# Low parts of the MLP's middle tiles on VectorE, and a quad's second pair of raw weights in the square tiles

## The chip, the cores and the metric

The kernel runs on one core of a Trainium2 chip. The metric is the device time of one launch in microseconds; the median of several runs counts. A core has TensorE (PE), which multiplies; VectorE (DVE), ScalarE (ACT) and GpSimd (POOL), which work elementwise; and SyncE (SP), which here only issues DMAs. POOL issues DMAs too: those that add into their target.

## The reference

Two layers of a decoder trunk on x (512 positions, 1024 features), all in float32:

```
for l in range(2):
    h = rms_norm(x, norm_mix_g[l])
    proj = h @ w_in[l]                      # then attention, short convolution, RWKV-7
    x = x + mixed @ w_out[l]
    h = rms_norm(x, norm_mlp_g[l])
    x = x + jnp.square(jax.nn.relu(h @ w_mlp_up[l])) @ w_mlp_down[l]    # 1024 -> 4096 -> 1024
return rms_norm(x, final_norm_g)
```

The change lies in the two lines of the MLP alone.

## The kernel before

Activations lie transposed: features on the 128 partitions, the 512 positions along the free axis, so x is eight tiles `x[j]` of 128x512. Every operand of a product is split into a high part (`hi`, a cast to the reduced format that PE multiplies, made by ACT) and a low part (`lo` = value - `hi`, made by DVE or POOL), and a product of two operands is three matmuls: hi*hi, hi*lo, lo*hi.

A layer has a mixing stage, whose order is written out by hand (`ORDER`) and which the change does not touch, and then the MLP. In the MLP a scheduler sets the order of each engine's instructions; every engine takes its own in that order. Tiles come from rings: a tag with `bufs` buffers, used in turn, where a new tile waits until the readers of the one that lay there before are done.

The MLP has 32 middle tiles (`mids`, 128 rows of the 4096 each). `up` makes the first four, `two(i0, i1)` makes two at a time by a Strassen-like scheme of seven products (p1 to p7) on half-size operands. Its sums of weights come by DMA: SP loads one block into `s` (L1476), POOL adds the other to it by an accumulating DMA (L1477). The products share banks: p1 goes to bank `pa`, is copied out by ACT (L1523, tile `p`), and p6, the third product, adds into the same bank. `square` and `kept` then finish a middle tile: DVE scales with the norm and clips (L1418), ACT squares (L1419) and casts to `mh` (L1409), and `ml` is the low part (L1410).

`down(h, js)` multiplies middle tiles 4h to 4h+3 with w_mlp_down and adds to x; it is called for each h in two halves, js = 0..3 and 4..7, alternating with the `two`s. There are three ways of it:

- plain (h = 0, 7, and some others): four `dn` products, weights through `weights` (ring `raw`, cast to `whi`, low part `wlo`, rings of WB = 3), the result added into x by DVE (L1683);
- for h in `BY_DMA` = (1, 3, 5) the odd j of it: ACT copies the result to a tile `dx` of tag `sq` (L1680), and POOL adds it into x by DMA (L1681). `sq`, with two buffers, is the tag that holds the squares of the norm elsewhere;
- for the halves in `DN_QUADS` (h = 2, 4, 6 in layer 0, h = 2, 4 in layer 1, both halves each, ten calls) `quad`, a scheme of products p1, p2, ... for two pairs of output tiles. For each pair i it loads two raw weight tiles `rawq` (ring `raw`), casts `whi`/`wlo` of them, and forms sums `s2q`, `s4q` of them, with `shi`/`slo`. Its products go to banks `qa`, `qb`, `qc`; ACT copies them out as `p1q`, `p5q`, `u2q`, `c1q` (L1600), and the next product into `qa` waits for `p1q`. One result goes into x by DMA (L1646, tile `c0q`).

So each quad group runs: last half of a plain `down` with dx tiles (h odd), `two`, quad half 0, `two`, quad half 1, `two`, `down` of the next h.

Of the kernel before, what the change touches and what calls it, by code (L numbers as in the profile page):

```python
# [10 lines left out]
F32 = mybir.dt.float32  # L11
# [5 lines left out]
ALU = mybir.AluOpType  # L17
# [6 lines left out]
P = 128  # L24
# [250 lines left out]
def tile_trunk(ctx: ExitStack, tc: tile.TileContext, xT, wts, prm_d, cst_d, lora_d, gup_d, lam_d, fin_d, hd_d, out):  # L275
    nc = tc.nc
    act, dve, pool = nc.scalar, nc.vector, nc.gpsimd
# [23 lines left out]
    wp = Pool(ctx.enter_context(tc.tile_pool(name="wp", bufs=2)), "wp")  # L301
# [3 lines left out]
    def psum(tag, bufs, name):  # L305
        return ps.tile([P, 512], F32, tag=tag, bufs=bufs, name=name)
# [23 lines left out]
    WB = 3  # L330
# [238 lines left out]
    for l in range(L):  # L569
# [826 lines left out]
        with ExitStack() as mx:  # L1396
# [7 lines left out]
            def kept(m):  # L1404

                i = len(mids)
                hi = fp.tile([P, S], F32R, tag="mh", bufs=RING, name=f"mh{l}_{i}")
                lo = fp.tile([P, S], F32R, tag="ml", bufs=RING, name=f"ml{l}_{i}")
                act.copy(hi, m)  # L1409
                (dve if i < 4 else pool).tensor_tensor(lo, m, hi.bitcast(F32), ALU.subtract)  # L1410
                mids.append((hi, lo))

            def square(cs, name, side=ALU.max):

                m = fp.tile([P, S], F32, tag="m", bufs=4, name=f"m{name}")
                for i, c in enumerate(cs):
                    q = slice(i * H, i * H + c.shape[1])
                    dve.scalar_tensor_tensor(m[:, q], c, 0.0, rs[:, q], side, ALU.mult)  # L1418
                act.activation(m, m, AF.Square)  # L1419
                kept(m)  # L1420
                return m
# [152 lines left out]
            def quad(h, half):  # L1574
# [3 lines left out]
                def split(src, pool_, tags, bufs, name):  # L1578
                    hi, lo = [pool_.tile([P, 4, P], F32R, tag=t, bufs=bufs, name=f"{t}{l}_{h}_{name}")[:, :src.shape[1]] for t in tags]
                    act.copy(hi, src)  # L1580
                    dve.tensor_tensor(lo, src, hi.bitcast(F32), ALU.subtract)
                    return hi, lo
# [23 lines left out]
                for i in range(2):  # L1606
                    j = 4 * half + 2 * i
                    n = f"{l}_{h}_{j}"
                    r0, r1 = [wp.tile([P, 4, P], F32, tag="raw", bufs=WB, name=f"rawq{n}_{c}") for c in range(2)]
                    for c, r in enumerate((r0, r1)):  # L1610
                        nc.sync.dma_start(r.rearrange("p k c -> p (k c)"),
                                          wts[wbase + NG_IN + NG_OUT + NG_UP + 8 * g + j + c, :, k0 * P:(k0 + 4) * P])
                    w0 = split(r0, wp, ("whi", "wlo"), WB, f"{j}a")
                    s = [fp.tile([P, 4, P], F32, tag=t, name=f"{t}q{n}") for t in ("s2", "s4")]
                    dve.tensor_tensor(s[0][:, :2], r1[:, 0::2], r1[:, 1::2], ALU.add)
                    dve.tensor_tensor(s[0][:, 2:], s[0][:, :2], r0[:, 0::2], ALU.subtract)
                    s12 = split(s[0], fp, ("shi", "slo"), 5, f"{j}b")
                    dve.tensor_tensor(s[1][:, :2], r0[:, 0::2], r1[:, 0::2], ALU.subtract)
                    dve.tensor_tensor(s[1][:, 2:], r0[:, 1::2], s[0][:, 2:], ALU.subtract)
                    s34 = split(s[1], fp, ("shi", "slo"), 5, f"{j}c")  # L1620
                    w22 = split(r1[:, 1::2], wp, ("whi", "wlo"), WB, f"{j}d")
                    pts = [psum(t, b, f"q{c}{n}")[:, :H] for c, t, b in zip("abc", (("rp", "rp", "at"), ("mm", "mm", "at"))[i],
                                                                          ((4, 4, 2), (2, 2, 2))[i])]
                    ab.append((j, w0, s12, s34, w22, pts))
                for step in ((0, 1), (2, 3), (5, 4), (6,)):
                    for j, w0, s12, s34, w22, (pa, pb, pc) in ab:
                        n = f"{l}_{h}_{j}"
# [28 lines left out]
            def down(h, js):  # L1656

                if (h, js[0] // 4) in DN_QUADS[l]:
                    quad(h, js[0] // 4)
                    return  # L1660
                g, k0 = h // 2, 4 * (h % 2)
                if h == 0 and js[0] == 0:
                    pts = [psum(("at", "mm")[j], 2, f"dn{l}_{h}_{j}") for j in js[:2]]
                    ws = [list(weights(wbase + NG_IN + NG_OUT + NG_UP + 8 * g + j, k0, k0 + 4)) for j in js[:2]]
                    for a, b in ((0, 3), (3, 4)):
                        for j, pt, w in zip(js, pts, ws):
                            for k in range(a, b):
                                (whi, wlo), (ahi, alo) = w[k], mids[k]
                                pe.matmul(pt, whi, ahi, start=(k == 0), stop=False)
                                pe.matmul(pt, whi, alo, start=False, stop=False)  # L1670
                                pe.matmul(pt, wlo, ahi, start=False, stop=(k == 3))
                    for j, pt in zip(js, pts):
                        dve.tensor_tensor(x[j], pt, x[j], ALU.add)
                    js = js[2:]
                for j in js:
                    pt = psum(*(("mm", 2), ("rp", 4))[j % 2], f"dn{l}_{h}_{j}")
                    mm3(pt, weights(wbase + NG_IN + NG_OUT + NG_UP + 8 * g + j, k0, k0 + 4), mids[4 * h:4 * h + 4], 4)
                    if j % 2 and h in BY_DMA:
                        t = wp.tile([P, S], F32, tag="sq", bufs=2, name=f"dx{l}_{h}_{j}")
                        act.copy(t, pt)  # L1680
                        pool.dma_start(x[j], t, accum_op=ALU.add)  # L1681
                    else:
                        dve.tensor_tensor(x[j], pt, x[j], ALU.add)  # L1683
                    if h == 2 * N_KG - 1 and j < NK - LATE:
                        norm_tile(j, f"m{l + 1}")
# [92 lines left out]
```

## Time and profile before

| | us |
|---|---|
| runs | 1240.45, 1240.89, 1245.29; median 1240.89 |
| profiled execution | 1243.22 |
| its span, first to last instruction | 1241.4 |
| PE busy | 1220.0 (98%) |
| DVE busy | 987.5 (80%) |
| ACT busy | 754.1 (61%) |
| POOL busy | 425.2 (34%) |
| mean granted PE clock | 0.995 |

The MLP of layer 0 lies at about 299 to 620 us, that of layer 1 at about 900 to 1241. Busy shares are means over stages; a wait of PE is what costs time. PE's matmuls are pipelined: a 128x256 matmul is shown with 0.28 us, but in an unbroken row the next one starts 0.119 us later (0.227 for 128x512). A row of the timeline has the start in us, the duration in us, engine, line, operation, output and inputs, and in brackets the engine's idle time before it with what ended it. In the list of waits the numbers are us in total, times, and the longest in us. The issue of a DMA and its landing are told apart: `us to landing` counts from the issue.

### The profile page before, as it was taken

The numbers are of one execution on the slowest core, as the hardware profiler recorded it, in microseconds if no ns is written. First come the engines' busy times: TensorE is split into PE (matmuls) and PEld (weight loads), VectorE is DVE, ScalarE is ACT, GpSimd is POOL, SyncE is SP. The second block draws the span as 40 slices with busy tenths as digits, with TensorE's granted clock in tenths as the row PEclk, the third lists the DMA queues.
The fourth block names the chain that finished last, engine by engine and source line by source line (L and its number), as shares of the span: only waits on it lengthen the run. The fifth ranks groups of instructions, "written<-read, shape, count | busy, mean of one in ns | idle before, by whom it ended". The sixth has DMA issues, their size and how long they took to land.

```text
span 1241.4 us, 27076 instructions
## 1 busy us (share of the span) xinstructions
PE 1220.0 (98%) x10090; PEld 1068.4 (86%) x10090; DVE 987.5 (80%) x1979; ACT 754.1 (61%) x1630; POOL 425.2 (34%) x546
## 2 busy tenths in 40 slices
PE   9999999999999999999999999999999999999997
PEld 7888788888989989889888888888889898999987
DVE  7787888879788988888866777787897889787654
ACT  7785755557566656556675656564675566665543
POOL 2264636331133332231126454554202323223111
PEclk9999999999999999899999999999999999999999
DMA  6523323135664775743335243322455656658322
GB/s 225 159 90 109 115 82 106 51 106 154 195 162 121 186 171 131 183 112 83 105 113 158 82 133 112 96 72 69 142 174 145 164 152 176 155 135 204 77 78 77
DMA packets 101844, 160.04 MB, mean 129 GB/s; under 512 B 23248, under 2 KB 27088, under 8 KB 101712
## 3 DMA queue, kind: packets, MB, share of 16 engines
q1 hardware_dynamic: 87168, 132.39, 33.8%
q0 software_dynamic: 13824, 25.17, 12.5%
q8 instruction: 79, 1.29, 0.5%
q10 hardware_dynamic: 720, 0.75, 0.2%
q14 instruction: 53, 0.43, 0.1%
HBM read 137.56 MB, written 9.18 MB: 118 GB/s over the span
## 4 chain that ended last, share of the span: by engine, by line
PE 87%; DVE 6%; ACT 3%; DMA 2%; issue 2%; POOLq 0%; POOL 0%; ACTq 0%; DVEq 0%
PE pj L288 22%; PE dn L288 14%; PE pa L288 12%; PE po L288 8%; PE pb L288 6%; PE qa L288 4%; PE dnF L288 4%; PE pc L288 3%; PE up L288 2%; PE qb L288 2%; PE sc L288 1%; DMA raw<-wts 1%; PE ptt L293 1%; PE pg L288 1%; DMA rawq<-wts 1%
## 5 line engine op out<-in xcount | busy, mean ns | idle before, releaser
L695 POOL TENSOR_TENSOR wlo<-raw,whi 128x512 fp32r<-128x512 f32 x84 | 112.4, 1339 | 198.1 <-ACT whi L683 164.6
L288 PE MATMUL pj<-ahim,whi 128*128 128x512 f32 x392 | 156.8, 400 | 0.0
L288 PE MATMUL pj<-ahim,wlo 128*128 128x512 f32 x392 | 156.4, 399 | 0.2 <-issue 0.2
L288 PE MATMUL pj<-alom,whi 128*128 128x512 f32 x392 | 156.0, 398 | 0.0
L683 ACT CAST whi<-raw 128x512 fp32r<-128x512 f32 x142 | 87.6, 618 | 70.6 <-PE pj L288 27.0
L1410 POOL TENSOR_TENSOR ml<-m,mh 128x512 fp32r<-128x512 f32 x56 | 82.8, 1529 | 131.3 <-ACT mh L1409 62.9
L1477 POOL DMA_DIRECT2D s<-wts x52 | 47.5, 914 | 222.2 <-DVE slo_p L1492 67.6
L288 PE MATMUL dn<-ml,whi 128*128 128x512 f32 x288 | 112.5, 391 | 0.3 <-DVE ml L1410 0.3
L288 PE MATMUL dn<-mh,whi 128*128 128x512 f32 x288 | 112.4, 390 | 0.2 <-ACT mh L1409 0.2
L288 PE MATMUL dn<-mh,wlo 128*128 128x512 f32 x288 | 112.2, 390 | 0.0
L1491 ACT CAST shi_p<-s 128x512 fp32r<-128x512 f32 x112 | 69.6, 621 | 56.6 <-PE pa L288 37.6
L288 PE MATMUL pa<-thi,shi_p 128*128 128x256 f32 x336 | 95.4, 284 | 1.8 <-ACT p L1523 1.6
L1492 DVE TENSOR_TENSOR slo_p<-s,shi_p 128x512 fp32r<-128x512 f32 x112 | 76.9, 694 | 25.2 <-ACT shi_p L1491 23.7
L288 PE MATMUL pa<-tlo,shi_p 128*128 128x256 f32 x336 | 94.8, 282 | 0.0
L288 PE MATMUL pa<-thi,slo_p 128*128 128x256 f32 x336 | 94.3, 281 | 0.0
L350 DVE TENSOR_TENSOR wlo<-raw,whi 128x512 fp32r<-128x512 f32 x86 | 71.1, 830 | 22.1 <-ACT whi L349 22.1
L288 PEld LDWEIGHTS pj<-alom,whi 128*128 128x128 f32 x392 | 73.9, 188 | 14.0 <-issue 0.5
L288 PEld LDWEIGHTS pj<-ahim,wlo 128*128 128x128 f32 x392 | 73.8, 188 | 13.8 <-issue 0.2
L288 PEld LDWEIGHTS pj<-ahim,whi 128*128 128x128 f32 x392 | 73.9, 188 | 13.7 <-issue 0.3
L349 ACT CAST whi<-raw 128x512 fp32r<-128x512 f32 x86 | 53.1, 619 | 51.5 <-PE dn L288 24.6
L1491 ACT CAST shi_p<-raw 128x512 fp32r<-128x512 f32 x84 | 52.2, 621 | 38.1 <-PE pb L288 19.5
L288 PEld LDWEIGHTS pa<-thi,shi_p 128*128 128x128 f32 x336 | 62.9, 187 | 3.0 <-ACT p L1523 2.7
(651 smaller groups left out, 3932.7 us busy)
## 6 DMA issues: line engine op xcount, KB each, us to landing
raw<-wts SPq DMA_DIRECT2D x323, 256.0 KB, 2.8
s<-wts SPq DMA_DIRECT2D x52, 256.0 KB, 3.6
s<-wts POOLq DMA_DIRECT2D x52, 256.0 KB, 4.6
rawq<-wts SPq DMA_DIRECT2D x40, 256.0 KB, 2.8
x<-dx POOLq DMA_DIRECT2D x24, 256.0 KB, 4.0
x<-c0q POOLq DMA_DIRECT2D x20, 256.0 KB, 4.2
qs<-dqhi SPq DMA_DIRECT2D x24, 128.0 KB, 3.3
ks<-dkhi SPq DMA_DIRECT2D x24, 128.0 KB, 3.6
```

Source lines behind the costliest of these rows:

```text
L288: ins = nc.tensor.matmul(*a, **k)
L293: ins = nc.tensor.transpose(*a, **k)
L349: act.copy(hi[:, :n], raw[:, :n])
L350: (pool if a and lean[0] else dve).tensor_tensor(lo[:, :n], raw[:, :n], hi[:, :n].bitcast(F32), ALU.subtract)
L683: yield act.copy(hi[:, k0:k1], raw[:, k0:k1])
L695: yield eng.tensor_tensor(lo[:, k0:k1], raw[:, k0:k1], hi[:, k0:k1].bitcast(F32), ALU.subtract)
L1410: (dve if i < 4 else pool).tensor_tensor(lo, m, hi.bitcast(F32), ALU.subtract)
L1477: pool.dma_start(t.rearrange("p k c -> p (k c)"), of[1], accum_op=ALU.add)
L1491: act.copy(hi, src)
L1492: dve.tensor_tensor(lo, src, hi.bitcast(F32), ALU.subtract)
```

## The change

Two lines change. The low part of every middle tile is now made by DVE (before: of the first four only). In a quad, the raw weights of the second pair (i = 1) come from the tag `sq` with its two buffers, and those of the first pair stay in `raw` with three. The additions into x by DMA stay as they are.

```diff
@@ kept
                 act.copy(hi, m)
-                (dve if i < 4 else pool).tensor_tensor(lo, m, hi.bitcast(F32), ALU.subtract)
+                dve.tensor_tensor(lo, m, hi.bitcast(F32), ALU.subtract)
                 mids.append((hi, lo))
@@ quad
                 for i in range(2):
                     j = 4 * half + 2 * i
                     n = f"{l}_{h}_{j}"
-                    r0, r1 = [wp.tile([P, 4, P], F32, tag="raw", bufs=WB, name=f"rawq{n}_{c}") for c in range(2)]
+                    r0, r1 = [wp.tile([P, 4, P], F32, tag=("raw", "sq")[i], bufs=(WB, 2)[i], name=f"rawq{n}_{c}") for c in range(2)]
```

The scheduler answers with another order on SP, ACT, DVE and POOL; PE's order is the same. In the rows below the layer's number is cut from the names and a running number is added: `rawq_2_4_0_5778` is the first raw tile (c = 0) of quad h = 2, pair j = 4; j = 0 and 2 are the two pairs of half 0, j = 4 and 6 those of half 1; `raw_4_6109` is a weight tile of the `down` of h = 3.

SP, layer 0, from the first half of quad h = 2 into the `two` behind its second half:

```order
+L1611 DMA rawq_2_4_0_5778<-wts 128x512
 L1611 DMA rawq_2_2_0_5477<-wts 128x512
-L1611 DMA rawq_2_4_0_5778<-wts 128x512
+L344 DMA raw_4_6109<-wts 128x512
 L1611 DMA rawq_2_2_1_5478<-wts 128x512
+L1611 DMA rawq_2_4_1_5779<-wts 128x512
 L1486 DMA raw_10_10_4_6012<-wts 128x512
-L1611 DMA rawq_2_4_1_5779<-wts 128x512
 L1611 DMA rawq_2_6_0_5807<-wts 128x512
+L1611 DMA rawq_2_6_1_5808<-wts 128x512
 L1486 DMA raw_10_24_4_6014<-wts 128x512
 L1476 DMA s_11_6016<-wts 128x512
```

The last raw tile, `rawq_2_6_1`, moves up to its neighbour (before, it stood five loads further down), and `rawq_2_2_0` goes behind `rawq_2_4_0`; `rawq_2_2_0` and `rawq_2_2_1` now wait for the DMA adds of `dx_1_5` and `dx_1_7`, whose tiles they take.

ACT, the end of `down` h = 1 and the start of the `two` in front of the quad's first half, before:

```order
L1580 CAST whi_2_0a<-rawq_2_0_0_5448 128x512
L1680 COPY dx_1_5_5231<-dn_1_5_5212 128x512
L1580 CAST whi_2_0d<-rawq_2_0_1_5449 128x256
L1580 CAST whi_2_2a<-rawq_2_2_0_5477 128x512
L1680 COPY dx_1_7_5273<-dn_1_7_5254 128x512
L1491 CAST shi_8_p_5400<-s_8_5398 128x512
L1523 COPY p_8_5312<-pa_8_5290 128x256
```

The same place on ACT in the changed kernel:

```order
L1680 COPY dx_1_5_5231<-dn_1_5_5212 128x512
L1571 CAST ahif_2_3916<-tb_2_1_5277 128x256
L1571 CAST ahif_3_3940<-tb_2_1_5277 128x256
L1580 CAST whi_2_0a<-rawq_2_0_0_5448 128x512
L1580 CAST whi_2_0d<-rawq_2_0_1_5449 128x256
L1680 COPY dx_1_7_5273<-dn_1_7_5254 128x512
L1580 CAST whi_2_2a<-rawq_2_2_0_5477 128x512
L1491 CAST shi_8_p_5400<-s_8_5398 128x512
L1523 COPY p_8_5312<-pa_8_5290 128x256
```

Both `dx` copies move up; `whi_2_2a`, which reads the tile that now waits for an add, still stands ahead of `p_8`, the copy of p1.

ACT, at the start of the quad's second half:

```order
+L1580 CAST shi_2_6b<-s2q_2_6_5815 128x512
 L1546 COPY c_9_5725<-pa_9_5620 128x256
-L1580 CAST shi_2_6b<-s2q_2_6_5815 128x512
 L1580 CAST shi_2_6c<-s4q_2_6_5816 128x512
 L1491 CAST shi_10_p_5956<-raw_10_10_0_5954 128x512
 L1419 ACTIVATE m_9_0_5747<-m_9_0_5747 128x512
+L1600 COPY p1q_2_4_5842<-qa_2_4_5804 128x256
+L1409 CAST mh_14_5750<-m_9_0_5747 128x512
 L1419 ACTIVATE m_9_1_5770<-m_9_1_5770 128x512
-L1409 CAST mh_14_5750<-m_9_0_5747 128x512
```

`p1q_2_4`, the copy that PE's next product into `qa` needs, moves ahead of one square and the casts of both middle tiles.

## Prediction

> **What bounds the kernel.** I read the page first, then the waits of TensorE, then the two halves of a quad in order of time.
>
> ```profile
> PE 1220.0 (98%) x10090; PEld 1068.4 (86%) x10090; DVE 987.5 (80%) x1979; ACT 754.1 (61%) x1630; POOL 425.2 (34%) x546
> PE qa L288 <- ACT p1q L1600: 8.8, 4, 3.0
> PE pa L288 <- ACT p L1523: 1.6, 2, 1.1
> ```
>
> PE is the bound, so the change is worth what it takes from or adds to PE's idle time, nothing else. The second and third lines are the list of PE's waits: 10.4 us of its idle lie in the MLP, in two places. `qa` is a product of a quad that waits until ScalarE has copied its bank out (`p1q`); `pa` is the third product of a pair of middle tiles, which adds into the bank of the first and so waits for the copy `p`. Both waits are for ACT.
>
> One of the four long ones cost more than its idle:
>
> ```profile
> core 0: us, PE busy (x) PEld busy (x) DVE busy (x) ACT busy (x) POOL busy (x), PEclk, DMA share, GB/s
> 506.00:509.00 3.00, 3.00 (x14) 3.00 (x15) 3.00 (x5) 1.94 (x6) 2.20 (x2) 0.50 0.49 163
> 509.00:512.00 3.00, 3.00 (x17) 3.00 (x16) 2.21 (x5) 1.15 (x3) 0.00 (x0) 0.54 0.52 161
> 1035.00:1038.00 3.00, 3.00 (x27) 3.00 (x27) 3.00 (x6) 1.94 (x6) 0.52 (x1) 1.00 0.50 178
> 505.93 0.58 PE L288 MATMUL qa<-dhi,shi_4b 128*128 128x256 f32 x1 [3.01 <-ACT p1q L1600]
> 1032.09 0.38 PE L288 MATMUL qa<-dhi,shi_4b 128*128 128x256 f32 x1 [2.61 <-ACT p1q L1600]
> ```
>
> After 3.01 us of idle the granted clock was 0.50 and 0.54 for 6 us: 31 matmuls started where 54 fit in the later, undisturbed stretch (27 in 3 us). 31 matmuls at 0.119 us each are 3.7 us, so this cost 2.3 us. After 2.61 us of idle the clock stayed at 1.00.
>
> [...]
>
> **First edit: 56 subtractions from POOL to DVE.**
>
> ```profile
> L1410 POOL TENSOR_TENSOR ml<-m,mh x56: 1284/1580/1869, 323.5 to 1188.5; 128x512 fp32r<-128x512 f32 x56
> L1410 DVE TENSOR_TENSOR ml<-m,mh x8: 682/684/693, 291.1 to 914.9; 128x512 fp32r<-128x512 f32 x8
> 355.57 2.86 POOL L1410 TENSOR_TENSOR ml<-m,mh 128x512 fp32r<-128x512 f32 x2
> 355.51 3.47 DVE L350 TENSOR_TENSOR wlo<-raw,whi 128x512 fp32r<-128x512 f32 x1
> 362.06 0.68 DVE L350 TENSOR_TENSOR wlo<-raw,whi 128x512 fp32r<-128x512 f32 x1
> L1562 DVE TENSOR_TENSOR ta<-m,ta 128x256 f32<-128x256 f32 x10 | 14.0, 1396 | 0.8 <-ACT m L1419 0.8
> L1596 DVE TENSOR_TENSOR x<-qa,x 128x256 f32<-128x256 f32 x20 | 8.3, 417 | 0.0
> ```
>
> The same line already runs on DVE for 8 tiles, at 0.684 us. So DVE gets 56 x 0.684 = 38 us more. Against it stands what POOL's work does to DVE now: during the pair at 355.57 one `wlo` took 3.47 us instead of 0.68, and the ten `ta` that lie beside such pairs took 1.40 us each instead of about 0.42 for that shape. That is 2.8 us and 1.0 us for a pair, against 1.4 us of new work; over all 56, DVE's excess beside POOL's `ml` in the timeline adds up to some 46 us. DVE ends about where it was, with shorter single steps, and no `ml` is late on PE's path. Price on PE: zero by itself; what covers it is DVE's own 20% of idle.
>
> One stall does hang on it. The stretched `wlo` of 355.51 holds a raw tile, SP's next load waits for it, then ACT's cast, then `p` behind the cast:
>
> ```profile
> 359.01 5.83 DMA raw<-wts
> 364.95 0.62 ACT L349 CAST whi<-raw 128x512 fp32r<-128x512 f32 x1 [3.32 <-DMA raw<-wts]
> 366.90 0.39 PE L288 MATMUL pa<-thi,shi_p 128*128 128x256 f32 x1 [1.10 <-ACT p L1523]
> ```
>
> With the stretch of 2.8 us gone and 0.6 to 1.2 us of `ml` put in, the load leaves some 2 us earlier, more than the 1.10 us that PE waited. I take both `pa` waits (1.6 us) as gone.
>
> **Second edit, second half of a quad.** Here the new place of the raw weights helps:
>
> ```profile
> 410.63 0.33 SPq L1611 DMA_DIRECT2D rawq<-wts  x1
> 413.44 0.43 DVE L1615 TENSOR_TENSOR s2q<-rawq 128x256 f32<-128x256 f32 x1 [1.03 <-DMA rawq<-wts]
> 419.09 0.63 ACT L1600 COPY p1q<-qa 128x256 f32<-128x256 f32 x2
> 418.68 0.28 PE L288 MATMUL qb<-dhi,slo_4b 128*128 128x256 f32 x1
> 419.50 0.39 PE L288 MATMUL qa<-dhi,shi_4b 128*128 128x256 f32 x1 [0.54 <-ACT p1q L1600]
> ```
>
> The last raw tile is issued at 410.63, behind SP's other loads, and everything that ACT does until `p1q` hangs on it. In the new order the load stands right behind its neighbour, waits only for the square tile's readers of the first half (done at 397.7 here), and lands some 10 us earlier; `p1q` also moves ahead of three casts and squares. Nothing else in the list is late: the fifth such half, whose load came early enough, has no wait. I take all four waits as gone: 8.8 us idle; plus, at each of the six waits, 0.16 us of drain and 0.1 us of restart that the idle does not count (418.68 to 419.50 is 0.82 us for a step of 0.12, and 0.54 was idle), 1.5 us; plus the 2.3 us of low clock. With the two `pa` waits: 8.8 + 1.6 + 1.5 + 2.3 = **14.2 us gained**.
>
> **Second edit, first half of a quad.** Here it costs. The square tiles still hold `dx` until its add by DMA has landed, and `rawq_2_2_0` waits for that:
>
> ```profile
> 380.37 0.33 SPq L1611 DMA_DIRECT2D rawq<-wts  x1
> 380.76 0.89 POOL L1477 DMA_DIRECT2D s<-wts  x1 [1.30 <-DVE tb L1564]
> 381.55 0.58 ACT L1680 COPY dx<-dn 128x512 f32<-128x512 f32 x1
> 382.54 0.87 POOL L1681 DMA_DIRECT2D x<-dx  x1 [0.89 <-ACT dx L1680]
> x<-dx POOLq DMA_DIRECT2D x1, 256.0 KB, 5.0
> rawq<-wts SPq DMA_DIRECT2D x40, 256.0 KB, 2.8
> 385.28 0.62 ACT L1580 CAST whi_2a<-rawq 128x512 fp32r<-128x512 f32 x1 [2.57 <-PE dn L288]
> 386.56 0.62 ACT L1491 CAST shi_p<-s 128x512 fp32r<-128x512 f32 x1 [0.17 <-PE pa L288]
> 387.08 0.37 ACT L1523 COPY p<-pa 128x256 f32<-128x256 f32 x1
> 387.92 0.28 PE L288 MATMUL pa<-thi,shi_p 128*128 128x256 f32 x1
> ```
>
> ACT's cast `whi_2a` stands ahead of `p`, which PE needs at 387.92. Now the load leaves at 380.37. In the changed kernel it leaves when the add has landed. `dx` is copied about 1.5 us earlier, but POOL issues the add only behind the `s` of 380.76, so at about 381.6, 0.9 earlier. Landing 5.0 later: 386.6. Load 2.8, and 0.1 for both wake-ups: 389.5. Cast, `shi` and `p` in a row, by their distances above 0.52 + 0.52 + 0.37 and 0.1 of wake-ups: 391.0. PE waits from 387.9 to 391.0, **3.1 us**. The other four quads are alike: their adds (466.31, 554.87, 993.97, 1078.11) went out 5.4, 5.4, 4.5 and 5.4 us ahead of that product and landed 4.1, 3.3, 3.3 and 4.2 later; they can go 0.8, 1.4, 2.3 and 0.7 earlier. Landing + 2.8 + 1.6 less the two gives 2.3, 0.9, 0.9 and 2.5 us.
>
> ```profile
> 554.87 0.88 POOL L1681 DMA_DIRECT2D x<-dx  x1 [3.08 <-ACT dx L1680]
> x<-dx POOLq DMA_DIRECT2D x1, 256.0 KB, 3.3
> 1078.11 0.86 POOL L1681 DMA_DIRECT2D x<-dx  x1 [0.68 <-ACT dx L1680]
> 1083.66 1.44 PE pa L288 x12
> x<-dx POOLq DMA_DIRECT2D x1, 256.0 KB, 4.2
> DMA to landing us min/median/max: 3.3/4.0/5.7
> ```
>
> (The rows are the third and the last of the five adds, each with its landing, the product of the last, from the chain of work, whose pieces begin 0.1 to 0.2 us after the matmul itself, and the landings of all 24 adds of this kind.) Together **9.7 us lost**. The bounds: a landing of 3.3 in all five leaves 0.9 to 1.4 each, 5 us; 5.7 in all gives 3.3 to 3.8 each, 18 us, and the low clock of 2.3 us after each gap over 3.0, up to 29 us. I keep each quad's own landing, since what else moves at that time is unchanged, and no low clock, the largest gap being at the edge.
>
> The second load of the pair, `rawq_2_2_1`, waits for the other `dx` and, on SP, behind a weight tile of the next group that waits for `s4q`. It lands about when DVE reaches it in the delayed order, and `p1q` behind it has 2.3 us to spare. Price zero; if that cover goes, `qa` waits.
>
> **Sum.** 1243.2 - 14.2 + 9.7 = 1238.7 by the profiled execution's own time (its span of 1241.4 and 1.8 around it), which is 2.3 us over the median of the runs shown, about what its low clock cost; a run without that gains 2.3 less, 1240.9 - 11.9 + 9.7 = 1238.7 as well. I take 1238.5.
>
> **Rivals.**
> - *The new waits are hidden or small.* For it: adds landed in 3.3 us twice; PE gains so much ahead of it only if the load comes before 388. Then the gain stands with 2 to 5 us lost: 1231 to 1234. [...] The rows say 3.3 to 5.7. Chance 0.28.
> - *Slower: the first halves wait over 3 us and lose the clock.* One mechanism, in the same place: adds that land in 5 us or more. It decides from about 20 us lost; four quads at 3.3 with 2.3 of clock each and one at 2 are 24: 1253. Against it: two of the five adds have POOL free and landed in 3.3. Chance 0.08.
> - *The second halves still wait*, because ACT or DVE has the new `ml` or another cast ahead of `p1q`: half of the 11 us stays, and with 9.7 lost it is 1243 to 1244, no change. Chance 0.12.
>
> **How the numbers follow.** My case, 5 to 15 us lost against 14, gives 1234 to 1244 and has 0.52. The range takes it, most of the first rival and the third: 1230 to 1245. The measurement tells about 0.5% from no change, 6.2 us: faster is under 1234.7, slower over 1247.1. Faster: the first rival and a little of mine, 0.32. Slower: 0.08. Same: 0.60.
>
> **What would show it.** Right: no POOL `ml`; DVE's `ta` of L1562 back at 0.42 us; the second halves' `qa` waits gone; in their place five waits of `pa` for `p` of L1523, 0.9 to 3.1 us long, some 9 us, with ACT's idle ahead of `whi_2a` put down to the DMA of `rawq`. Wrong: no such waits (the adds land in time), or granted clock of 0.5 behind them, or `qa` still waiting for `p1q`.

## The result and the profile after

The changed kernel is slower: 1251.34 us median of five runs (1246.99 to 1252.86) against 1241.11 for the kernel before, measured beside it; by the ratio 1.0063 [1.0036, 1.0091]. That is above the predicted range (1230 to 1245), and slower where the forecast, 1238.5, was a little faster. The profiled execution took 1252.86 us, 9.6 us more than the profiled one of before, with a span of 1251.0.

The lines that answer to those of before: the busy time on the page, the list of TensorE's waits, and two groups of instructions (duration in ns, least/median/most).

```profile
PE 1225.1 (98%) x10090; PEld 1074.0 (86%) x10090; DVE 977.8 (78%) x2035; ACT 753.9 (60%) x1630; POOL 345.2 (28%) x490
PE pa L288 <- ACT p L1523: 14.3, 5, 4.0
L1410 DVE TENSOR_TENSOR ml<-m,mh x64: 677/684/695, 291.5 to 1198.0; 128x512 fp32r<-128x512 f32 x64
L1562 DVE TENSOR_TENSOR ta<-m,ta x10: 413/418/421, 355.0 to 1080.9; 128x256 f32<-128x256 f32 x10
```

The waits `qa` for `p1q` are gone. In their place stand five waits of `pa` for `p`, the copy of p1, one in front of each first half of a quad, as forecast in kind. They are longer than forecast: 14.3 us instead of 9.7. DVE has 56 more instructions and is 9.7 us less busy, since what stood beside GpSimd's pairs is short again: the ten `ta` take 0.418 us instead of 1.40.

The first of the five places in time (POOL, SP, ACT, PE), and then the third, the only short one:

```profile
379.83 0.88 POOL L1477 DMA_DIRECT2D s<-wts  x1 [5.24 <-DVE s2q L1616]
380.39 1.22 POOL L1681 DMA_DIRECT2D x<-dx  x1
385.81 0.33 SPq L1611 DMA_DIRECT2D rawq<-wts  x1
389.20 0.62 ACT L1580 CAST whi_2a<-rawq 128x512 fp32r<-128x512 f32 x1 [4.26 <-DMA rawq<-wts]
390.24 0.36 ACT L1523 COPY p<-pa 128x256 f32<-128x256 f32 x1
390.66 0.58 PE L288 MATMUL pa<-thi,shi_p 128*128 128x256 f32 x1 [3.49 <-ACT p L1523]
...
555.30 0.87 POOL L1681 DMA_DIRECT2D x<-dx  x1 [14.34 <-ACT ahif L1571]
558.70 0.33 SPq L1611 DMA_DIRECT2D rawq<-wts  x1
561.33 0.62 ACT L1580 CAST whi_2a<-rawq 128x512 fp32r<-128x512 f32 x1 [1.05 <-DMA rawq<-wts]
562.79 0.38 PE L288 MATMUL pa<-thi,shi_p 128*128 128x256 f32 x1 [0.28 <-ACT p L1523]
```

The chain is the predicted one: the add of `dx` lands, only then SP issues the load, ACT's cast waits for it, `p` stands behind the cast, PE waits for `p`. In the first place the add goes out 0.56 us behind POOL's accumulating DMA of `s`; in the third no such DMA is ahead of it. The landings of these five adds, each from the list of DMAs of its own moment (the first and the third), and the two kinds on the page:

```profile
x<-dx POOLq DMA_DIRECT2D x1, 256.0 KB, 5.0
x<-dx POOLq DMA_DIRECT2D x1, 256.0 KB, 3.3
rawq<-wts SPq DMA_DIRECT2D x40, 256.0 KB, 3.1
x<-dx POOLq DMA_DIRECT2D x24, 256.0 KB, 4.8
```

What follows a long wait is seen in stretches of 8 us from the end of each of the five waits (PE's instructions in brackets; behind POOL's the granted clock):

```profile
core 0: us, PE busy (x) PEld busy (x) DVE busy (x) ACT busy (x) POOL busy (x), PEclk, DMA share, GB/s
390.60:398.60 8.00, 7.94 (x45) 7.94 (x46) 5.00 (x12) 2.92 (x8) 0.00 (x0) 0.64 0.40 132
478.70:486.70 8.00, 7.94 (x55) 7.94 (x56) 5.95 (x13) 3.77 (x9) 0.00 (x0) 0.81 0.41 133
562.70:570.70 8.00, 7.91 (x66) 7.91 (x67) 6.70 (x15) 4.43 (x10) 0.00 (x0) 1.00 0.45 122
1005.10:1013.10 8.00, 7.95 (x45) 7.95 (x46) 5.00 (x12) 2.93 (x8) 0.00 (x0) 0.64 0.43 133
1093.40:1101.40 8.00, 7.97 (x44) 7.97 (x45) 4.96 (x11) 2.92 (x7) 0.00 (x0) 0.61 0.39 131
```

Behind the short wait 66 matmuls start in 8 us at full clock; behind the four long ones 45, 55, 45 and 44 do. That is 75 matmuls of 0.119 us less, 8.9 us. The distances between the starts themselves, against the same steps in a kernel without these waits (e6_dxm below; TensorE's order is the same), give 9.5.

| product `pa` at | wait forecast | idle measured | delay from start to start | lost to the clock in the next 8 us | landing of the add, taken / measured |
|---|---|---|---|---|---|
| 390.66 | 3.1 | 3.49 | 3.65 | 2.64 | 5.0 / 5.0 |
| 478.76 | 2.3 | 3.12 | 3.27 | 1.40 | 4.1 / 4.8 |
| 562.79 | 0.9 | 0.28 | 0.44 | 0.09 | 3.3 / 3.3 |
| 1005.15 | 0.9 | 4.04 | 4.19 | 2.59 | 3.3 / 4.9 |
| 1093.43 | 2.5 | 3.33 | 3.48 | 2.79 | 4.2 / 4.9 |
| sum | 9.7 | 14.3 | 15.0 | 9.5 | 19.9 / 22.9 |

The same reckoning by starts for the six waits of the kernel before gives 11.5 us of delays and 3.2 in the 8 us after each, 2.7 of these behind one wait. So 14.6 us went and 24.5 came, 9.9 net, which is the 9.6 us between the two profiled executions to within half a microsecond.

### The profile page after: what moved, and what is told of

It is laid out like the page before. It is cut to its first block, busy times and chain, and to the rows that moved or that the text cites. A ratio compares the mean times of both kernels' runs of the same rounds, so it can differ in the third digit from the quotient of the medians.

```text
span 1251.0 us, 26957 instructions
## 1 busy us (share of the span) xinstructions
PE 1225.1 (98%) x10090; PEld 1074.0 (86%) x10090; DVE 977.8 (78%) x2035; ACT 753.9 (60%) x1630; POOL 345.2 (28%) x490
## 4 chain that ended last, share of the span: by engine, by line
PE 83%; DMA 5%; DVE 5%; issue 3%; ACT 3%; POOL 0%; SPq 0%; POOLq 0%; ACTq 0%; DVEq 0%
PE pj L288 21%; PE pa L288 12%; PE dn L288 10%; PE po L288 8%; PE pb L288 5%; PE qa L288 5%; PE dnF L288 4%; PE pc L288 3%; PE qb L288 2%; DMA x<-dx 2%; PE sc L288 1%; DMA rawq<-wts 1%; PE ptt L293 1%; PE qc L288 1%; PE up L288 1%
## 5 line engine op out<-in xcount | busy, mean ns | idle before, releaser
L288 PE MATMUL pa<-thi,shi_p 128*128 128x256 f32 x336 | 98.5, 293 | 14.3 <-ACT p L1523 14.3
L288 PEld LDWEIGHTS pa<-thi,shi_p 128*128 128x128 f32 x336 | 65.7, 195 | 15.9 <-ACT p L1523 15.6
L350 DVE TENSOR_TENSOR wlo<-raw,whi 128x512 fp32r<-128x512 f32 x86 | 58.6, 684 | 20.9 <-ACT whi L349 20.9
L288 PEld LDWEIGHTS pa<-thi,slo_p 128*128 128x128 f32 x336 | 66.4, 197 | 0.0
```

Of the source, the lines that this page charges most:

```text
L288: ins = nc.tensor.matmul(*a, **k)
L350: (pool if a and lean[0] else dve).tensor_tensor(lo[:, :n], raw[:, :n], hi[:, :n].bitcast(F32), ALU.subtract)
```

## The experiments

The medians below are of runs beside the kernel before on the same chip, which had 1243.04 us in the first group (e1_ml, e3_half1, e4_dve57, e6_dxm), 1241.27 in the second (e2_sq, e5_dve5, e7_dvecast, e10_nos), 1242.17 in the third (e8_idle2, e9_idle4) and 1242.13 in the last (e11_fill).

**The first edit alone (e1_ml).**

```diff
-                    r0, r1 = [wp.tile([P, 4, P], F32, tag=("raw", "sq")[i], bufs=(WB, 2)[i], name=f"rawq{n}_{c}") for c in range(2)]
+                    r0, r1 = [wp.tile([P, 4, P], F32, tag="raw", bufs=WB, name=f"rawq{n}_{c}") for c in range(2)]
```

> The first edit alone: all low parts of the middle tiles on VectorE, the quads' raw weights as in the kernel before. Theory (the loss comes from the square tiles alone): no new wait of pa for p in the first halves; the waits of qa for p1q stay (8 to 10 us of idle, since the last raw tile still comes late), the two pa waits of 1.6 us go; 1238 to 1241 us against 1241. Rival A (the low parts on VectorE delay what stands ahead of p): pa waits of 3 us in the first halves here too, 1247 us or more.

Measured: 1231.04 us (1229.77 to 1233.14), ratio 0.991 [0.9889, 0.993]. This expectation missed. The second halves' waits are almost gone without the second edit. From the list of waits and from the timelines of DVE and ACT at the second half of the first quad:

```profile
PE qa L288 <- ACT p1q L1600: 0.5, 2, 0.3
412.73 0.43 DVE L1615 TENSOR_TENSOR s2q<-rawq 128x256 f32<-128x256 f32 x1 [1.10 <-DMA rawq<-wts]
415.65 0.36 ACT L1600 COPY p1q<-qa 128x256 f32<-128x256 f32 x1
416.83 0.63 ACT L1419 ACTIVATE m<-m 128x512 f32<-128x512 f32 x1 [0.81 <-DVE m L1418]
```

The vector engine still waits for the load of the last raw tile, 1.10 us here against 1.03 before. What has changed is what stands on ACT between the sums and `p1q`. The order of ACT in this kernel, at that place:

```
L1580 CAST shi_2_6c<-s4q_2_6_5816 128x512
L1491 CAST shi_10_p_5956<-raw_10_10_0_5954 128x512
L1600 COPY p1q_2_4_5842<-qa_2_4_5804 128x256
L1419 ACTIVATE m_9_0_5747<-m_9_0_5747 128x512
L1580 CAST whi_2_6d<-rawq_2_6_1_5808 128x256
L1409 CAST mh_14_5750<-m_9_0_5747 128x512
```

Before, both squares (1.15 us), both casts `mh` (1.12) and `whi_6d` (0.40), 2.7 us in all, came ahead of `p1q`. It ran 3.9 us behind the first product of the half (419.09 against 415.23); here it runs 1.2 us behind it (415.65 against 414.44). Where the low part `ml` is made changes the scheduler's order on ACT, and that, not an earlier load, takes this wait away. In the three places where the wait was 2.6 to 3.0 us, `p1q` moves up by 4.0 to 5.0 us against the half's first product. The same 2.7 of it are the order; the rest, 1.3 to 2.3, is the last raw tile, which lands earlier there although its edit is missing. So the order is the larger part of this gain; by itself it is seen only in the first place.

**The second edit alone (e2_sq)**, with the low parts back on GpSimd:

```diff
-                dve.tensor_tensor(lo, m, hi.bitcast(F32), ALU.subtract)
+                (dve if i < 4 else pool).tensor_tensor(lo, m, hi.bitcast(F32), ALU.subtract)
```

> The second edit alone: rawq_*_0 and rawq_*_1 of a half's second pair in the sq tiles, the low parts of the late middle tiles still on GpSimd. The page of the first edit alone showed qa<-p1q waits of 0.5 us where before had 8.8, so the gain that the prediction gave to this edit may belong to the other one. Theory A (as the prediction put it: the raw load of the second halves comes too late, and the sq tiles let it start sooner): qa<-p1q is gone here as well, and the five first-half pa<-p waits stand at 12 to 18 us in all with three or four low-clock stretches of some 2.4 us; time 1245 to 1254. Theory B (the second halves' wait is one of the order in which the scalar engine takes p1q, and only the first edit changes it): qa<-p1q stays at 6 to 9 us in all beside the first-half waits; time 1255 to 1264. Should the adds go out later behind GpSimd's own low parts, the first-half waits are longer than in the changed kernel (over 15 us), by either theory.

Measured: 1255.55 us (1252.08 to 1258.6), 1.0111 [1.0094, 1.0129]. No `qa` wait is left, as theory A has it, and the waits in front of the five first halves are all there, 16.0 of the 17.2 us below. The time lies a little above A's range and just inside B's, but the `qa` waits that B rests on are missing.

```profile
PE pa L288 <- ACT p L1523: 17.2, 6, 4.6
```

So each edit alone takes the second halves' waits away, and together they cannot take them away twice. That the earlier load alone does it is not shown: in e2_sq the last raw tile lands some 12 to 16 us earlier against the half's first product, but `p1q` has moved up on ACT as well, behind one square instead of two squares, two casts `mh` and `whi_6d`. What the second edit costs is seen in both places: with its gain it is still 14 us over the kernel before, and on top of the first edit, where almost no wait is left to gain, it is 20 us (1251.34 against 1231.04; 19 by the ratios).

**Without the wait for the tile.** Four kernels keep both edits and remove the wait of the loads for `dx` in different ways. e6_dxm gives the `dx` of j = 5 and 7 other tiles, with the adds by DMA kept:

```diff
-                        t = wp.tile([P, S], F32, tag="sq", bufs=2, name=f"dx{l}_{h}_{j}")
+                        if j < 4:
+                            t = wp.tile([P, S], F32, tag="sq", bufs=2, name=f"dx{l}_{h}_{j}")
+                        else:
+                            t = fp.tile([P, S], F32, tag="m", bufs=4, name=f"dx{l}_{h}_{j}")
```

> Both edits and the same adds by DMA, but the dx tiles of the halves ahead of a quad lie in the ring of the middle tiles' squares (tag m, four buffers) instead of the square tiles. Only what the load waits for changes. Theory: the loads leave early, no wait in the first halves, 1226 to 1231 us. Rival D (the load is late for another reason, SP's order or the DMA engines' load by the adds): first-half waits of 1 us and more stay, 1235 or more.

e4_dve57 adds j = 5 and 7 by DVE out of the bank, so there is no `dx`:

```diff
-                    if j % 2 and h in BY_DMA:
+                    if j in (1, 3) and h in BY_DMA:
```

> Both edits; in the halves of down ahead of a quad the two dx tiles are gone and VectorE adds their results into x from the bank (12 adds of 0.69 us in all: j = 5 and 7 of h = 1, 3, 5 in both layers). Theory: the square tiles are free, the first halves have no wait; 1226 to 1231 us. Rival A: no change against the changed kernel, about 1250. Rival C (VectorE has no room for 8 us more there): pa or qa waits of about 1 us each, 1232 to 1238.

e3_half1 uses the square tiles in the second halves only:

```diff
-... tag=("raw", "sq")[i], bufs=(WB, 2)[i], ...
+... tag=("raw", "sq")[i * half], bufs=(WB, 2)[i * half], ...
```

> Both edits, but only the second half of a quad takes its second pair of raw weights from the square tiles; the first half's stay in the raw ring. Theory: the adds of dx have landed long before the second half needs its tiles, so the waits of the first halves (15 us with their restarts, 9.5 us of low clock behind them) go and the waits of the second halves stay away: 1226 to 1231 us. Rival A: first halves still wait, 1243 us or more. Rival B (the second halves need the first half's tiles moved too, so that the raw ring is free early): qa waits come back, about 1238 to 1241.

e5_dve5 adds only j = 5 by DVE (`if j in (1, 3, 7) and h in BY_DMA`):

> Both edits; of the two sums that go through the sq tiles by DMA ahead of a first half (j = 5 and 7) only j = 5 is added by the vector engine from PSUM instead, so rawq_*_2_0's tile is free when its load is due, and rawq_*_2_1 still waits for the add of j = 7. Theory: only the first load's wait for its tile matters, because whi_2a is cast from it and stands ahead of p on the scalar engine; no pa<-p wait over 0.5 us, 1228 to 1231 as with both sums on the vector engine (1228.35). Rival: the second load (cast whi_2d and the sums s2q, which stand further back) holds the engines in the same way; pa<-p or p1q waits of 1 to 3 us in four or five places, 1235 to 1248.

| | median (range), us | ratio to before |
|---|---|---|
| e6_dxm | 1229.25 (1228.07 to 1229.92) | 0.9892 [0.987, 0.9913] |
| e4_dve57 | 1228.35 (1228.05 to 1229.19) | 0.9886 [0.9865, 0.9908] |
| e3_half1 | 1229.51 (1229.36 to 1230.54) | 0.9896 [0.9875, 0.9918] |
| e5_dve5 | 1229.45 (1227.53 to 1231.63) | 0.9908 [0.9894, 0.9921] |

All four are some 22 us faster than the changed kernel, and none has a wait of `pa` or `qa` in its list. e5_dve5 frees only the first load's tile and is as fast, so the first load's wait is the one that counts, and its rival falls. e6_dxm is the sharpest: the same sums go by the same DMAs, and only the place of `dx` differs. In it ACT's cast waits for PE again and not for a load, and `p` is copied 4.2 us earlier than in the changed kernel:

```profile
384.04 0.62 ACT L1580 CAST whi_2a<-rawq 128x512 fp32r<-128x512 f32 x1 [2.36 <-PE dn L288]
386.06 0.37 ACT L1523 COPY p<-pa 128x256 f32<-128x256 f32 x1
```

With the conflict out of the way the second edit is worth 1.5 to 2.7 us on the first one (three kernels of the first group). That is less than half a per cent, and the intervals of the ratios overlap with that of e1_ml.

**The neighbour on POOL's queue (e10_nos).** The order of all engines stays; four accumulating DMAs of `s` are left out.

```diff
-                    pool.dma_start(t.rearrange("p k c -> p (k c)"), of[1], accum_op=ALU.add)
+                    if name == "s1" or i0 not in (10, 14):
+                        pool.dma_start(t.rearrange("p k c -> p (k c)"), of[1], accum_op=ALU.add)
```

> Both edits; left out are the accumulating DMAs of the tiles s3 for groups 10 and 14 in both layers (the second addend of that sum is missing, four DMAs of 256 KB), which stand on GpSimd's queue directly ahead of the add of j = 5. All engines' orders are the same but for these four. In the changed kernel the add of j = 5 goes out 0.56 to 0.62 us behind that DMA, and the raw load that waits for it 5.0 to 5.4 us after; where no such DMA stands ahead (the third place) it was 3.4 us. Theory: the neighbour on the queue is what makes the add land late; without it the load goes out 3.3 to 4.2 us after the add and the add itself some 0.5 us earlier, so the four waits of 3.1 to 4.0 us shrink by 1.4 to 2.5 us each to 1 to 2.3, their low-clock stretches go, and the time is 1234 to 1241. Rival: the add lands in 5 us by itself (what it reads and writes, not its neighbour); the waits shrink by the 0.5 us of earlier issue alone, to 2.6 to 3.5 us, and the time is 1244 to 1250.

Measured: 1232.13 us (1231.54 to 1233.34), 0.9926 [0.9914, 0.9937], even below what the theory gave. Its waits (the lines behind the edit are numbered one higher), the first and the second place, and the landing of the add in the first place and in the second:

```profile
PE pa L288 <- ACT p L1524: 2.8, 5, 1.4
379.79 0.87 POOL L1682 DMA_DIRECT2D x<-dx  x1 [5.09 <-ACT ahif L1572]
386.95 0.62 ACT L1581 CAST whi_2a<-rawq 128x512 fp32r<-128x512 f32 x1 [2.17 <-DMA rawq<-wts]
463.76 0.87 POOL L1682 DMA_DIRECT2D x<-dx  x1 [5.37 <-ACT ahif L1572]
469.81 0.62 ACT L1581 CAST whi_2a<-rawq 128x512 fp32r<-128x512 f32 x1 [1.07 <-DMA rawq<-wts]
...
x<-dx POOLq DMA_DIRECT2D x1, 256.0 KB, 4.1
x<-dx POOLq DMA_DIRECT2D x1, 256.0 KB, 3.3
```

The five landings are 4.1, 3.3, 3.3, 3.3 and 3.3 us; with the neighbour the four that have one took 5.0, 4.8, 4.9 and 4.9. From the add's issue to ACT's cast it is 7.2 and 6.1 us in these two places, and was 8.8 and 8.3. The raw load gets shorter too, which the theory had not counted: 2.6 to 2.7 us from its issue to the cast in the four places, where it took 3.3 to 3.7. Whether the add suffers because it stands behind the other on the queue, or because the two share the DMA engines, this does not tell apart; both go with the neighbour. One thing in the changed kernel speaks for sharing: the adds of j = 7 have no POOL DMA in the 4 us ahead of them, but in these four places SP issues the raw load 0.2 to 0.7 us behind them, and they landed in 4.1 to 5.0 us. In the third place, where the load left 2 us ahead, and in all five of e10_nos, where it left 0.9 to 2.0 us ahead, it was 3.3.

**The cast on another engine (e7_dvecast).**

```diff
-                    act.copy(hi, src)
+                    if half == 0 and name == "2a":
+                        dve.tensor_copy(hi, src)
+                    else:
+                        act.copy(hi, src)
```

> Both edits, loads as late as in the changed kernel; only the five casts whi_2a of a first half's second pair (which wait for the late load) run on the vector engine instead of ScalarE, so that p1's copy no longer stands behind them on ScalarE. The order on the other engines is the same. Theory (the wait reaches TensorE through ScalarE's order alone): pa<-p falls from 23.3 us idle to under 3 us if nothing on the vector engine that stands behind the cast is due at once, 1229 to 1236; whatever wait is left moves to the vector engine's products for the following tiles (slo, c0) and shows under a vector-engine releaser. Rival 1 (the vector engine's order holds TensorE just as ScalarE's did): five waits of 2 to 4 us with a DVE releaser instead, 1245 to 1254. Rival 2 (the load is late for its own product as well): waits on whi_2a or wlo_2a themselves.

Measured: 1240.84 us (1238.27 to 1244.01), 0.9992 [0.9981, 1.0003], between the theory and the first rival. TensorE's waits, then DVE and ACT at the first place:

```profile
PE qa L288 <- ACT p1q L1603: 8.0, 8, 1.3
390.38 0.43 DVE L1581 CAST whi_2a<-rawq 128x512 fp32r<-128x512 f32 x1 [7.34 <-PE pc L288]
396.88 0.43 DVE L1618 TENSOR_TENSOR s2q<-rawq 128x256 f32<-128x256 f32 x1 [1.75 <-DMA rawq<-wts]
398.01 0.62 ACT L1583 CAST shi_2b<-s2q 128x512 fp32r<-128x512 f32 x1 [4.04 <-DVE s2q L1619]
399.81 0.36 ACT L1603 COPY p1q<-qa 128x256 f32<-128x256 f32 x1
```

(What had been idle at `pa` is 14.3 us by the list of waits, not 23.3.) The waits of `pa` for `p` are gone, so it is ACT's order that brings the late load to PE there. But now DVE stands still for 7.34 us at the cast (the row names PE, but the load landed at 390.29, just ahead of the cast), and the quad's own sums come late: `shi_2b` waits for `s2q`, `p1q` stands behind it, and eight `qa` waits of up to 1.3 us take the place. Both raw tiles are really late; moving one reader moves the wait.

**The clock.** Two kernels were to make idle stretches of chosen length in the kernel without waits (e6_dxm) by repeating one copy:

```diff
                 act.copy(p1, pa)
+                if i0 in ((9, 13, 17), (9, 13))[l]:
+                    for _ in range(17):              # 10 in e8_idle2
+                        act.copy(p1, pa)
```

> A test of the clock on the version without waits (both edits, the sums of j = 5 and 7 staged in four m tiles, 1229.25 us): ScalarE's copy p1 is repeated 10 times in five groups (9, 13 and 17 of the first layer, 9 and 13 of the second), each repeat writing the same values again, so TensorE's matmuls pa<-thi,shi_p behind it wait. At an estimated 0.26 us for a repeat and some 0.7 us of slack, five idle stretches of 1.5 to 2.5 us. Theory (only stretches of about 3 us and more cost clock): no stretch at a lower clock, 1229 + 5 x 2 = 1237 to 1243 us. Rival (any idle stretch costs clock in proportion): tails of 1 to 2 us behind each, 1244 to 1252.

> The same with 17 repeats: at an estimated 0.26 us each five idle stretches of 3.3 to 4.5 us. Theory (such a stretch is followed by up to some 3 us at a lower clock that costs up to 2.8 us, as behind four of the five stretches of the changed kernel): 1229 + 5 x 4 + 3 to 5 tails of 1.4 to 2.8 = 1254 to 1262 us. Rival (the tails in the changed kernel come from something else than the idle time): five gaps with tails under 0.3 us, 1247 to 1251.

Measured: 1231.4 us (1230.9 to 1231.89) and 1235.68 (1235.21 to 1236.61). Both are inconclusive: the scheduler put other products ahead of the one that waits, and neither list of waits has a `pa` for `p`. The longest idle stretch of TensorE in the MLP is 0.3 us, so there was nothing to test; what made the second one some 6 us slower than e6_dxm is not shown. (The stretches at a lower clock in the changed kernel are 3.4 and 6.8 us long, not "some 3"; the last section has them.)

The other way round it worked (e11_fill): in the changed kernel, TensorE is given matmuls to do during the four long waits.

```diff
+                s2w = both(s2, "p6")
+                if i0 in (8, 12):
+                    for _ in range(28):
+                        pe.matmul(pc, w1[0][:, 0], acts[0][0][:, :H], start=True, stop=False, skip_group_check=True)
-                product(pa, both(s2, "p6"), smm(1), False)
+                product(pa, s2w, smm(1), False)
```

(`w1` is p1's pair of weight tiles.)

> Both edits; TensorE is kept at work in the four long first-half waits: ahead of the product pa (p6) of groups 8 and 12 in both layers stand 28 matmuls of 128x256 (at the 0.119 us of the pb rows 3.34 us) into the bank of pc, whose content is overwritten afterwards; they need nothing that is late. TensorE's order is otherwise the same, some casts on ScalarE swap neighbours. In the changed kernel the four waits delay TensorE by 3.65, 3.27, 4.19 and 3.48 us, and the 8 us after each lose another 2.64, 1.40, 2.59 and 2.79 us to a lower clock. Theory (the low clock follows the idle time, not the place): the fill takes the place of the wait, so the delays stay at 3.3 to 4.2 us each, but the 9.4 us of low clock go: 1251.3 - 9.4 = 1241.9, between 1239 and 1245. Rival (the slower matmuls after the waits come from something else there, say operands that arrive late): 1248 to 1253.

Measured: 1244.71 us (1241.71 to 1248.48), 1.0019 [1.0005, 1.0034]. The list of waits, and 8 us that begin close behind the first and the third long wait:

```profile
PE pa L288 <- ACT p L1524: 1.6, 4, 0.6
390.60:398.60 8.00, 7.63 (x64) 7.63 (x65) 7.72 (x17) 4.91 (x12) 0.00 (x0) 1.00 0.46 153
1003.00:1011.00 8.00, 7.69 (x64) 7.70 (x65) 7.78 (x17) 4.91 (x11) 0.00 (x0) 1.00 0.39 132
```

The fill of 13.4 us and the 1.6 us of waits left make 15.0, no less than the 14.3 us of waits in the changed kernel; and yet the kernel is 6.6 us faster by the medians (0.44%, 5.5 us, by the ratios), since the granted clock stays at 1.00 in the 8 us behind all four fills, where it was 0.64, 0.81, 0.64 and 0.61 behind the four waits of the changed kernel. The low clock thus follows the idle time in these places. The median lies at the theory's upper end, 2.8 us above its middle; the mean clock of the changed kernel's five runs varied from 0.989 to 0.994, and their times from 1246.99 to 1252.86 us.

## Why the prediction was wrong, point by point

*The bound.* Right. PE's waits, and the clock behind them, account for the difference to within half a microsecond.

*First edit, DVE's load.* Right: DVE ended no busier, `ta` is at 0.42 us, and no `ml` is late. **Its price of zero on PE beyond the two `pa` waits was wrong.** The price was made from durations, and the edit's effect lies for the larger part in the order: it moves `p1q` ahead on ACT. The first edit alone brings 0.9%, 11 to 12 us.

*Second edit, second halves, 14.2 us gained.* The size was right (all six waits went, 14.6 us with their clock), the cause only half: the second edit alone takes the `qa` waits away (e2_sq), though with another order on ACT too, and it is not needed for it (e1_ml). The step "everything that ACT does until `p1q` hangs on it" left out that some 2.7 us of squares and casts stood there too. Since the prediction was for both edits together, this alone did not move the number; it made the second edit look as if it paid for itself.

*Second edit, first halves, 9.7 us lost.* The mechanism was right in place, releaser and number of waits, and the term is the one that failed, in two steps.

- "I keep each quad's own landing, since what else moves at that time is unchanged." It was not: pulled forward, the add comes directly behind POOL's DMA of `s` in four of five places, and lands in 4.8 to 5.0 us where 3.3 to 5.0 was taken. In three of the four it had stood 1.6 to 1.8 us behind such a DMA before (landings of 5.0, 4.1 and 4.2). In the fourth, at 1005.15, it had stood 3.2 us behind (landing 3.3), and there the wait came out 3.1 us longer than forecast. The landings make 3.0 of the 4.6 us between 9.7 and 14.3; the rest is the load, from whose issue to ACT's cast 2.6 to 3.7 us passed where 2.9 was taken. The prediction had the add and the `s` in one fence and reckoned only when the one could follow the other. The start-to-start delays are 0.7 us more than the idle, an allowance that the prediction made for the waits that went and not for those that came.
- "And no low clock, the largest gap being at the edge." Four of the five waits were over 3 us, and all four lost clock, 9.5 us together. The row of before (3.01 us idle, clock 0.50) was on the table. The length of the gap alone did not decide (in e2_sq the clock stayed at 1.00 after 3.33 us and was 0.79 after 2.78; the last section), so "at the edge" was no reason for nothing.

With 15.0 and 9.5 in place of 9.7 the sum is 1243.2 - 14.2 + 24.5 = 1253.5, against 1252.86 profiled. The prediction's own bounds, 5 to 29 us lost, hold these 24.5; its range took only 5 to 15.

*The second load of the pair.* Its price of zero was right: the changed kernel has no `qa` wait. So was its condition: in e7_dvecast, where the delay of `pa` no longer covers it, the `qa` waits come.

*The rivals.* What happened is the slower one: four waits of over 3 us that lose the clock, priced at 24 us and 1253. It was given 0.08 because two adds of before had landed in 3.3 us; of these one still did. The first rival, waits that are hidden or small, did not occur: no landing of these five was under 3.3 us, and four took 4.8 to 5.0. The third rival, second halves that still wait, did not occur.

## What to carry to other kernels

When a buffer is shared with a tile that a DMA reads, its release is that DMA's landing, and a landing read from the old trace holds only while the DMA keeps its neighbours (at 1005.15 the 3.3 us of before became 4.9); price it with the slowest landing seen once anything ahead of it on its queue moves. A wait near the length at which the clock has been seen to drop (3.01 us in the kernel before, 2.78 in e2_sq) should be carried into the sum with the clock's price: four of the five waits here paid it, 1.4 to 2.8 us each. And two edits that remove the same wait should be tried one by one: here one of them was all of the gain (1231.04 us alone), and the other all of the loss; the lowest median seen, both edits with the sums of j = 5 and 7 on the vector engine, is 1228.35, with three other ways of removing the conflict within 1.2 us of it.

## What the runs showed of the hardware that was not expected

*Idle stretches of about the same length did not cost the clock the same here; it mattered where they lay in periods of 3.413 us.* In e2_sq three of the waits of `pa` were followed by these stretches, after 3.33, 2.78 and 3.31 us of idle time:

```profile
480.30:488.30 8.00, 7.98 (x67) 7.98 (x68) 6.00 (x13) 3.73 (x8) 0.00 (x0) 1.00 0.41 133
1006.50:1014.50 8.00, 7.97 (x54) 7.97 (x55) 5.83 (x13) 3.66 (x8) 0.00 (x0) 0.79 0.38 133
1093.70:1101.70 8.00, 7.90 (x44) 7.91 (x45) 5.00 (x11) 2.92 (x8) 0.00 (x0) 0.62 0.37 131
480.32 0.39 PE L288 MATMUL pa<-thi,shi_p 128*128 128x256 f32 x1 [3.33 <-ACT p L1523]
1006.53 0.39 PE L288 MATMUL pa<-thi,shi_p 128*128 128x256 f32 x1 [2.78 <-ACT p L1523]
```

After 3.33 us the clock stayed at 1.00, after 2.78 it was 0.79 over 8 us, after 3.31 it was 0.62; in the kernel before it stayed at 1.00 after 2.61.

The records of the granted clock show where the stretches lie. In the changed kernel the granted clock is 0.50 from 389.60 for 6.83 us, from 478.35 for 3.41, and from 1004.00 and 1092.74 for 6.83 each; in e2_sq it is so from 393.23 and 1007.63 for 3.41 us each and from 1092.96 for 6.83, in the MLP of the kernel before only from 504.91 for 6.83. Every length is once or twice 3.413 us, and the distances between the starts are 26, 154 and 26 of these periods in the changed kernel, and 180 and 25 in e2_sq. So in these traces the changes of the clock within each kernel lie on an even grid: from the first to the last of the starts in the changed kernel it is 703.14 us, 206 periods of 3.413 us. Stretches of one period on that grid, the first from the kernel before and the others from e2_sq:

```profile
501.50:504.91 3.41, 1.41 (x12) 1.21 (x11) 3.41 (x8) 3.01 (x7) 0.00 (x0) 1.00 0.25 77
475.15:478.56 3.41, 1.84 (x16) 1.63 (x14) 0.00 (x0) 0.00 (x0) 0.88 (x1) 1.00 0.48 117
478.56:481.97 3.41, 1.65 (x13) 1.65 (x14) 2.42 (x5) 2.23 (x6) 0.00 (x0) 1.00 0.23 42
1004.22:1007.63 3.41, 1.10 (x9) 1.10 (x10) 1.88 (x4) 2.20 (x5) 0.00 (x0) 1.00 0.37 73
1007.63:1011.04 3.41, 3.41 (x19) 3.41 (x18) 1.47 (x3) 0.94 (x3) 0.00 (x0) 0.50 0.60 205
```

In the kernel before, the period of the 3.01 us wait has TensorE busy for 1.41 us, and the clock drops at its end. In e2_sq the wait of 3.33 us is split between two periods, in which TensorE is still busy for 1.84 and 1.65 us, and the clock stays. The wait of 2.78 us lies almost whole in one, with 1.10 us busy, and the next period runs at 0.50. The three kernels have twelve waits of 1.9 us and more: the eight that lost the clock have a period with 2.0 to 3.2 us of idle time in it, and the four that did not have at most 1.8 in any. Where between the two the limit lies, these waits do not show. Full clock came back after one period at 478.35 in the changed kernel and at 1007.63 in e2_sq, with TensorE busy for 3.00 and 3.41 us of it, and after two at 504.91 in the kernel before and at 389.60, 1004.00 and 1092.74 in the changed kernel, where it was busy for 2.40, 2.35, 2.25 and 2.73 us of the first. An estimate from these numbers: a wait between some 2 and 3.5 us can go either way, as it falls on the grid.

*The add of `dx` landed later where another accumulating DMA of 256 KB went out 0.56 to 0.62 us ahead of it:* in the changed kernel it took 4.8 to 5.0 us in four such places. With the first left out (e10_nos) it took 3.3 in three of them and 4.1 in the fourth.
